# Six split-weight buffers per ring at one offset, constants in common tiles, a smaller DMA scratch, a re-priced plan, and short inverse roots on GpSimd

## Chip, core and metric

The kernel runs on one core of a Trainium2 chip. The time is the device time of one execution in microseconds (us). Lower is better. One execution of it was also recorded by the hardware profiler, and the rows below come from that recording.

## What is computed

Two layers of a hybrid block over 256 latent tokens and 256 context tokens, model width 1024, all in float32. Each layer normalises the tokens with a modulated RMS norm, projects them once, feeds three token mixers, merges these by gates, projects, and runs an MLP of width 4096. The last layer needs the latent tokens alone.

```python
for l in range(DEPTH):                                   # DEPTH = 2
    mod = silu(c) @ w_mod[l] + b_mod[l]                  # shifts, scales, gates
    h_lat, h_ctx = rms_norm(x, norm1_g[l]) * (1 + sc1) + sh1, ...   # 256 tokens each
    z = split_cols(h @ w_in[l])                          # one projection for all branches
    y_da  = rms_norm(differential attention over [lat, ctx]) # per head, q and k rms-normed, rope
    y_gla = rms_norm(gated linear attention, both ways) * silu(gate)
    y_na  = neighbourhood attention on a 64-wide grid (q, k rms-normed)
    m = sum(sigmoid(g_i) * (y_i @ w_br_i)) @ w_out[l]
    x = x + g1 * m
    x = x + g2 * (relu(h2 @ w_ff1[l]) ** 2) @ w_ff2[l]   # h2: second modulated norm
    if l < DEPTH - 1: the same for ctx                   # 512 columns in layer 0, 256 in layer 1
```

## The kernel before

All weights come from HBM in pieces of 128x1024 float32 (512 KB), in one planned list. For each piece `load_weights` issues a transfer on SyncE's queue (SP) into one of five `raw` buffers. `split_weights` then makes two float32r halves of it: ScalarE (ACT) copies it to `wh`, VectorE (DVE) subtracts to give `wl`. A product takes three float32r matmuls: high by high, high by low, low by high. There are five `wh` and five `wl` buffers (`NW`), each 1152 wide, and the piece's 1024 columns start at an offset that goes by the buffer: 0 for pieces planned without `shift`, and `SHIFTS` = 16, 48, 64, 80, 112 columns for those with it. Pieces with `shift` are those of layer 1 that TensorE (PE) holds as the stationary operand, with 256 columns moving: 24 of the gates, 12 of the branches, 8 of the output projection, 32 each of ff1 and ff2, 108 in all. In each of them 8 blocks by 3 products are 24 matmuls.

The order of the instructions is made while the program is built. `Lane` hands every instruction to `Plan.note`, which adds up planned times (`FIXED`, `PER`, `LATENCY`, `SLOWER`), and `drive` runs the tasks (first norm, modulation, norms, attention branches, the weight stream) by when their inputs will be there by that plan. Each engine then runs its own list in order. So a changed price in the plan changes the order on all engines.

An inverse root is made by `rsqrt` on DVE: a bit trick and three Newton steps, after one instruction that scales and adds EPS. It stands at the five norms over the model width (`norm_rms`; 4 columns in the first one, 2 in the others), at GLA's heads (`heads_rms` with 8 columns), at the end of each differential-attention head (`head_end`; 4 columns in layer 0, 2 in layer 1), and at the q and k of both softmax attentions (16 or 32 columns).

In each layer the job `ga` loads three tables: `sb` (gains and lambdas) and two `gl` tiles (decay bias and decay weights `a2`), on SP's queue. ACT and DVE split the second `gl` tile (tile `a`) and the decay projection `gat`, and PE needs both for the decays. The residual stream `x` is loaded again in layer 0 by eight transfers on GpSimd's (POOL's) queue.

Of the kernel before, what the change touches and what calls it, by code (L numbers as in the profile page):

```python
# [11 lines left out]
F32 = mybir.dt.float32  # L12
# [7 lines left out]
P = 128  # L20
# [16 lines left out]
OFF_GATE = (4640, 5664, 6688)  # L37


RS = -1.0 / 8192.0  # L40

SA_BMOD, SA_N1, SA_N2, SA_W = 0, 48, 56, 64
SB_GQ, SB_GQP, SB_GK, SB_GKP = 0, 64, 128, 192
SB_LAM = 256
SB_SUB, SB_GN, SB_NQ, SB_NK, SB_W = 512, 513, 514, 515, 516


INF = 1e9
# [12 lines left out]
AHEAD = 2
# [7 lines left out]
MOD1_AFTER = (0, "ff1", 0)  # L69


FIXED = {"DVE": 0.068, "ACT": 0.1, "Pool": 0.045, "PE": 0.005}
PER = {"DVE": 1.04e-3, "ACT": 0.833e-3, "Pool": 2.3e-3, "PE": 1 / 2400}
LATENCY = {"DVE": 0.13, "ACT": 0.2, "Pool": 0.13, "PE": 0.25, "DMA": 2.0}
DMA_PER_BYTE = 2.9 / 2 ** 20


class Plan:
# [13 lines left out]
    def note(self, lane, op, args, kw):  # L92
        aps = [x for x in args[1:] if isinstance(x, bass.AP)]
        aps += [v for k, v in kw.items() if isinstance(v, bass.AP) and k != "accum_out"]
        out = args[0]
        width = lambda x: math.prod(x.shape[1:])
        n = width(out)
        if op == "dma_start":
            us = n * out.shape[0] * 4 * DMA_PER_BYTE
            self.now["DMA"] = max(self.now["DMA"], self.now["PE"]) + us  # L100
            self.wr[out.tensor.name] = max(self.now["DMA"], self.rd.get(out.tensor.name, 0.0) + us) + LATENCY["DMA"]
            return
        if lane == "PE":
            passes = 2 if op == "transpose" else 1 if aps[0].dtype == F32R else 4
            us = max(n, 64) * passes * PER["PE"] * out.shape[0] * aps[0].shape[0] / P ** 2 * SLOWER[passes] + FIXED["PE"]
            shape = aps[0].shape[0], out.shape[0]
            kind = shape, passes
            us += SWITCH * (shape != self.kind[0]) + SWITCH * (kind != self.kind and kind == ((P, P), 1))
            self.kind = kind
        else:  # L110
            n = max(n, max((width(x) for x in aps), default=0))
            sb = lane == "DVE" and op in ("tensor_copy", "tensor_scalar", "memset") and \
                not any(x.tensor.name.startswith("ps") for x in aps)
            us = FIXED[lane] + n * PER[lane] * (0.5 if sb else 1)
            pointers = sum(width(x) == 1 for x in aps) if n > 1 else 0
            if lane == "ACT" and REFINE:
                us += 0.09 * (pointers + ("accum_out" in kw)) - (0.042 if aps[0].tensor.name.startswith("ps") else 0)
            elif lane == "ACT" and "accum_out" in kw:
                us += 0.09
            elif lane == "DVE" and REFINE and pointers:  # L120
                us += 0.06
        start = max(self.now[lane], self.ready(aps), self.rd.get(out.tensor.name, 0.0))
        end = start + us
        self.now[lane] = end
        for x in aps:
            self.rd[x.tensor.name] = max(self.rd.get(x.tensor.name, 0.0), end)
        for x in [out] + ([kw["accum_out"]] if "accum_out" in kw else []):
            self.wr[x.tensor.name] = end + LATENCY[lane]

# [30 lines left out]
def build(nc, tc, ctx, a):  # L160
# [63 lines left out]
    def after(key):  # L224
        return lambda: 0.0 if key in done else INF
# [23 lines left out]
        else:  # L249
            V.tensor_tensor(out, x, x, MULT)  # L250

    def rsqrt(dst, x, tmp):

        V.tensor_scalar(dst.bitcast(I32), x.bitcast(I32), -0.5, 1597463007.0, MULT, ADD)
        n = x.shape[-1]
        for thr in (3.0, 12.0, 768.0):
            if n <= 2:
                for i in range(n):
                    c = slice(i, i + 1)
                    V.scalar_tensor_tensor(tmp[:, c], dst[:, c], dst[:, c], x[:, c], MULT, MULT)  # L260
            else:
# [6 lines left out]
    raws, parts, held = {}, {}, []  # L270

    def plan_w(src, width=2048, shift=False):
# [10 lines left out]
    def split_weights(force=False):  # L283
# [14 lines left out]
        if held[-1]:  # L298
            w = []
            for c in cs:  # L300
                w.append((u("xw", dtype=F32R), u("xw", dtype=F32R)))
                S.activation(w[-1][0], s[:, c], AF.Copy)
                V.tensor_tensor(w[-1][1], s[:, c], w[-1][0].bitcast(F32), SUB)
        else:

            i = SHIFTS[st["ring"]] if plan[n][1] else 0
            st["ring"] = (st["ring"] + 1) % NW
            h, lo = [buf(t, t, 1152, NW, F32R)[:, i:i + 1024] for t in ("wh", "wl")]
            S.activation(h, s, AF.Copy)
            V.tensor_tensor(lo, s, h.bitcast(F32), SUB)  # L310
            w = [(h[:, c], lo[:, c]) for c in cs]
# [298 lines left out]
    def heads_rms(zs, width):  # L610
# [100 lines left out]
    def da_attn(L, lam_init, y):  # L711
        l, q, k, v = L["l"], L["dq"], L["dk"], L["dv"]
        nq = len(L["qt"])
        yield after((l, "dq"))
        sb = L["sb"]
        tab = []
        for (g0, g1, f) in ((SB_GQ, SB_GQP, RS * HD ** -0.5), (SB_GK, SB_GKP, RS)):
            t = small("ropet", [P, 2, 2, HD])
# [16 lines left out]
        V.tensor_scalar(gain, sb[:, SB_SUB:SB_SUB + 1], 0.5 * (1.0 - lam_init) * RS, None, MULT)  # L735
# [79 lines left out]
        def head_end(h, left):  # L815
# [8 lines left out]
            V.tensor_scalar(ss, ss, 1.0 / P, EPS, MULT, ADD)  # L824
            rsqrt(r, ss, tmp)
# [113 lines left out]
    def gla(L, y):  # L939
# [151 lines left out]
    def start(l, h):  # L1091
# [431 lines left out]
    def first_norm():  # L1523
# [18 lines left out]
        trif = u("trif").rearrange("p (r c) -> p r c", r=4)  # L1542
        S.dma_start(trif, a["tri"])
# [54 lines left out]
def _layout(i):  # L1598
# [52 lines left out]
    sb[:, :, SB_SUB] = i["da_subln_g"]  # L1651
    sb[:, :, SB_GN] = i["gla_gn_g"]
    sb[:, :, SB_NQ] = np.concatenate([i["na_qn_g"]] * 2, 1)
    sb[:, :, SB_NK] = np.concatenate([i["na_kn_g"]] * 2, 1)
# [29 lines left out]
```

## Time and profile before

| what | value |
|---|---|
| median of 3 runs | 1524.97 us (1524.93 to 1526.73) |
| profiled execution, own time | 1523.46 us |
| its span | 1521.3 us |
| PE busy | 1487.3 us (98%) |
| DVE, ACT, POOL busy | 1068.6, 707.2, 20.8 us |
| mean granted TensorE clock | 0.994 |

The profiled execution is 1.5 us under the median, and 2.2 us of it lie outside its span. Busy time is a union of records, and a matmul's record reaches past the start of the next one, so the pace of PE is read from the distance between starts.

### The profile page before, as it was taken

Reading aid. Unit: us, or ns where it says so; the run is one execution under the profiler, and the core shown is the slowest. Engines: PE = TensorE matmul, PEld = TensorE weight load, DVE = VectorE, ACT = ScalarE, POOL = GpSimd, SP = SyncE. Lnnn points to the kernel's source line nnn. Section 1 sums busy time; section 2 is a strip of 40 time slices with the busy share of each in tenths; the row PEclk is TensorE's granted clock in tenths of the full one; section 3 lists DMA queues with packets and bytes.
Section 4 is the critical chain, followed back from the end, with each engine's and each line's share of the span. In section 5 each row is a group of like instructions: output and inputs, shape, how many; then the busy total and the mean of one; then the engine's idle time right before and its main releaser. Section 6 shows DMA issues by size and latency. Waiting matters only on the chain.

```text
span 1521.3 us, 24039 instructions
## 1 busy us (share of the span) xinstructions
PE 1487.3 (98%) x9340; PEld 1279.3 (84%) x9340; DVE 1068.6 (70%) x2242; ACT 707.2 (46%) x1243; POOL 20.8 (1%) x30
## 2 busy tenths in 40 slices
PE   7899999999999999999999999999999999999999
PEld 5788878888877888988888888888887889989999
DVE  5788796698986376698876334877867685786543
ACT  4444435553345433623324252464466455477632
POOL 0100000000000100100000000000000000000000
PEclk9999999999999999999999999999999999999999
DMA  9533331157522422366885222324224325346662
GB/s 364 189 108 104 97 112 56 56 187 224 185 80 67 139 97 84 132 219 199 262 274 173 97 97 91 111 70 133 84 77 138 130 92 186 128 164 202 208 201 78
DMA packets 77793, 216.66 MB, mean 142 GB/s; under 512 B 9072, under 2 KB 12528, under 8 KB 77680
## 3 DMA queue, kind: packets, MB, share of 16 engines
q1 hardware_dynamic: 74880, 210.28, 41.7%
q10 hardware_dynamic: 2160, 2.76, 0.6%
q0 software_dynamic: 640, 2.10, 0.4%
q8 instruction: 73, 1.20, 0.3%
q14 instruction: 40, 0.33, 0.1%
HBM read 214.05 MB, written 1.05 MB: 141 GB/s over the span
## 4 chain that ended last, share of the span: by engine, by line
PE 75%; DVE 17%; ACT 3%; DMA 3%; issue 2%; SPq 0%; ACTq 0%; DVEq 0%
PE psg L141 63%; PE pss L141 11%; DVE wl L141 4%; DVE dump L141 2%; DVE z L141 2%; DVE wm L141 2%; DMA wm<-w_mod 2%; ACT wh L141 1%; DVE ss L141 1%; DMA gl<-gl 1%; DVE hn L141 1%; DVE h L141 1%; DVE S L141 1%; DVE st L141 0%; DMA raw<-w_tok 0%
## 5 line engine op out<-in xcount | busy, mean ns | idle before, releaser
L141 DVE TENSOR_TENSOR wl<-raw,wh 128x1024 fp32r<-128x1024 f32 x290 | 354.2, 1228 | 163.1 <-ACT wh L141 162.7
L141 PE MATMUL psg<-h,wh 128*128 128x256 f32 (+1 forms) x1808 | 444.4, 337 | 3.9 <-ACT z L141 2.0
L141 ACT ACTIVATE wh<-raw 128x1024 fp32r<-128x1024 f32 x290 | 301.7, 1053 | 195.3 <-PE psg L141 186.2
L141 PEld LDWEIGHTS psg<-h,wh 128*128 128x128 f32 x1808 | 305.6, 190 | 43.6 <-issue 5.5
L141 PE MATMUL psg<-wh,h 128*128 128x512 f32 (+1 forms) x1056 | 333.3, 391 | 0.1
L141 PE MATMUL psg<-h,wl 128*128 128x256 f32 (+1 forms) x904 | 301.4, 333 | 0.5 <-DVE wl L141 0.5
L141 PE MATMUL psg<-act,wh 128*128 128x256 f32 (+1 forms) x1056 | 249.0, 329 | 0.0
L141 PEld LDWEIGHTS psg<-wh,h 128*128 128x128 f32 x1056 | 197.7, 188 | 43.9 <-issue 2.5
L141 PE MATMUL psg<-wl,h 128*128 128x512 f32 (+1 forms) x528 | 204.3, 387 | 0.0
L141 PEld LDWEIGHTS psg<-act,wh 128*128 128x128 f32 x1056 | 178.3, 188 | 18.8
L141 PEld LDWEIGHTS psg<-h,wl 128*128 128x128 f32 x904 | 171.1, 189 | 18.1 <-DVE wl L141 0.8
L141 PE MATMUL psg<-act,wl 128*128 128x256 f32 (+1 forms) x528 | 173.9, 329 | 0.0
L141 DVE SCALAR_TENSOR_TENSOR dump<-wm,cb 128x512 f32<-128x512 f32 x160 | 107.8, 686 | 19.4 <-DMA wm<-w_mod 17.0
L141 PEld LDWEIGHTS psg<-wl,h 128*128 128x128 f32 x528 | 99.6, 189 | 18.9
L141 PEld LDWEIGHTS psg<-act,wl 128*128 128x128 f32 x528 | 99.4, 188 | 9.4
L141 PE MATMUL psg<-y,wh 128*128 128x512 f32 (+1 forms) x384 | 96.4, 342 | 0.0
L141 DVE TENSOR_TENSOR act<-r,act 128x256 fp32r<-128x256 f32 (+1 forms) x65 | 36.2, 557 | 66.9 <-ACT act L141 66.9
L141 DVE SCALAR_TENSOR_TENSOR x<-psg,mod,x 128x256 f32<-128x256 f32 x96 | 43.1, 479 | 56.7 <-PE psg L141 56.7
L141 ACT ACTIVATE r<-psg 128x256 f32<-128x256 f32 (+1 forms) x63 | 30.0, 476 | 95.8 <-PE psg L141 95.8
L141 PEld LDWEIGHTS psg<-y,wh 128*128 128x128 f32 x384 | 64.3, 189 | 7.3 <-issue 0.7
L141 PE MATMUL psg<-sp,wh 128*128 128x256 f32 (+1 forms) x304 | 66.5, 315 | 1.7 <-ACT sp L141 1.4
L141 DVE SCALAR_TENSOR_TENSOR wm<-wm,cb 128x512 f32<-128x512 f32 x96 | 66.2, 690 | 2.7
(223 smaller groups left out, 1679.4 us busy)
## 6 DMA issues: line engine op xcount, KB each, us to landing
raw<-w_ff SPq DMA_DIRECT2D x128, 512.0 KB, 4.4
wm<-w_mod SPq DMA_DIRECT2D x192, 256.0 KB, 4.0
raw<-w_tok SPq DMA_DIRECT2D x72, 512.0 KB, 4.0
raw<-w_gate SPq DMA_DIRECT2D x48, 512.0 KB, 3.9
raw<-w_br SPq DMA_DIRECT2D x24, 512.0 KB, 3.5
raw<-w_out SPq DMA_DIRECT2D x16, 512.0 KB, 3.8
tb<-natb SPq DMA_DIRECT2D x16, 192.0 KB, 4.1
x<-xc SPq DMA_DIRECT2D x8, 256.0 KB, 4.1
```

Source lines behind the costliest of these rows:

```text
L141: r = f(*args, **kw)
```

## The change

Six things are edited together. The rings get a sixth `wh` and `wl` buffer, and all shifted pieces start at column 16. Room for them comes from a DMA scratch of 1 KB in place of 4 KB, and from the differential-attention tables, which move to tiles of the common pool (`tabs`, `few`, and the 512 columns `sbd` of the table `sb`). `inv_rms` takes the place of `rsqrt`: up to 8 columns it is one DVE instruction and one GpSimd `pow` with exponent -0.5, above that Newton as before. The `gl` tiles are loaded from ACT's queue. The copy of the constant `tri` is made in layer 0's GLA, not at the start. The plan's prices change (a DMA's latency from 2.0 to 3.3, the factor of one-pass matmuls from 1.057 to 1.0622, a price for `pow`).

```diff
-RS = -1.0 / 8192.0
+RS = 1.0 / 8192.0
-NU, NRAW, NW, NWM = 64, 5, 5, 4
+NU, NRAW, NW, NWM = 64, 5, 6, 4
-SHIFTS = 16, 48, 64, 80, 112
+SHIFT = 16
-SWITCH, SLOWER = 0.095, {1: 1.057, 2: 1.0, 4: 1.03}
+SWITCH, SLOWER = 0.095, {1: 1.0622, 2: 1.01, 4: 1.05}
-LATENCY = {"DVE": 0.13, "ACT": 0.2, "Pool": 0.13, "PE": 0.25, "DMA": 2.0}
+LATENCY = {"DVE": 0.13, "ACT": 0.2, "Pool": 0.13, "PE": 0.25, "DMA": 3.3}
...
+            if ALU.pow in args:
+                us = 0.35 + 0.185 * n
...
-    def rsqrt(dst, x, tmp):
+    def inv_rms(dst, x, n, tmp, src=None):
+
+        src = x if src is None else src
+        m = x.shape[-1]
+        if m <= 8:
+            V.tensor_scalar(x, src, RS * RS / n, RS * RS * EPS, MULT, ADD)
+            G.tensor_tensor(dst, x, nhalf[:, :m], ALU.pow)
+            return
...
-            i = SHIFTS[st["ring"]] if plan[n][1] else 0
-            st["ring"] = (st["ring"] + 1) % NW
+            i = SHIFT if plan[n][1] else 0
             h, lo = [buf(t, t, 1152, NW, F32R)[:, i:i + 1024] for t in ("wh", "wl")]
...
-            L["sb"] = spool.tile([P, SB_W], F32, name=nm("sb"), tag="sb", bufs=1)
-            SP.dma_start(L["sb"], a["sb"][l])
+            L["sb"] = spool.tile([P, SB_W - 512], F32, name=nm("sb"), tag="sb", bufs=1)
+            SP.dma_start(L["sb"], a["sb"][l, :, 512:])
+            L["sbd"] = u("sbd")
+            SP.dma_start(L["sbd"], a["sb"][l, :, :512])
             ab, a2 = u("gl"), u("gl")
             for i, t in enumerate((ab, a2)):
-                SP.dma_start(t, a["gl"][l, i])
+                S.dma_start(t, a["gl"][l, i])
...
-        V.tensor_copy(tri, trif)
+        trif.append(u("trif").rearrange("p (r c) -> p r c", r=4))
+        S.dma_start(trif[0], a["tri"])
...
-    nc = bacc.Bacc("TRN2", target_bir_lowering=False, num_devices=1, dynamic_dma_scratch_size=4096)
+    nc = bacc.Bacc("TRN2", target_bir_lowering=False, num_devices=1, dynamic_dma_scratch_size=1024)
```

What this does to the order is shown at three places. The first is SP's queue in layer 0, where the first token projection is running and the tables of `ga` are due; the name in brackets is the semaphore that the issue waits for, and transfers take the eight DMAHW semaphores in turn. Before:

```order
L141 DMA raw_603<-w_tok 128x1024 [waits DMAHW3_49,DMAHW0_49,DVE_49]
L141 DMA wm_614<-w_mod 128x512 [waits DMAHW4_49]
L141 DMA wm_616<-w_mod 128x512 [waits DMAHW5_49]
L141 DMA wm_618<-w_mod 128x512 [waits DMAHW6_49]
L141 DMA wm_620<-w_mod 128x512 [waits DMAHW7_49]
L141 DMA sb_650<-sb 128x516 [waits DMAHW0_49]
L141 DMA gl_652<-gl 128x512 [waits DMAHW1_49,PE_49]
L141 DMA gl_653<-gl 128x512 [waits DMAHW2_49,PE_49]
```

And of the change, at the same place:

```order
L144 DMA raw_595<-w_tok 128x1024 [waits DMAHW3_49,DMAHW0_49,DVE_49]
L144 DMA raw_607<-w_tok 128x1024 [waits DMAHW4_49,DMAHW1_49,DVE_49]
L144 DMA wm_615<-w_mod 128x512 [waits DMAHW5_49]
L144 DMA wm_617<-w_mod 128x512 [waits DMAHW6_49]
L144 DMA wm_619<-w_mod 128x512 [waits DMAHW7_49]
L144 DMA wm_621<-w_mod 128x512 [waits DMAHW0_49]
L144 DMA sb_646<-sb 128x4 [waits DMAHW1_49]
L144 DMA sbd_648<-sb 128x512 [waits DMAHW2_49,PE_49]
```

One more `raw` transfer stands ahead of the modulation's weights (`wm`), and the two `gl` transfers have left the queue. They now stand on ACT. This is ACT at that place before, from the first of the four evacuations `z` of that projection:

```order
L141 ACTIVATE z_631<-psg_338 128x512 [waits PE_49]
L141 ACTIVATE z_636<-psg_368 128x512 [waits PE_49,Activation_49]
L141 ACTIVATE z_641<-psg_372 128x512 [waits PE_49,Activation_49]
L141 ACTIVATE z_648<-psg_376 128x512 [waits PE_49]
L141 ACTIVATE wh_665<-raw_336 128x1024 [waits Activation_49]
L141 ACTIVATE a_153_656<-gl_653 96x512 [waits DMAHW2_49]
L141 ACTIVATE gat_708<-psg_671 96x512 [waits PE_49]
```

And of the change:

```order
L144 ACTIVATE z_629<-psg_331 128x512 [waits PE_49]
L144 ACTIVATE z_634<-psg_350 128x512 [waits PE_49,Activation_49]
L144 ACTIVATE z_639<-psg_354 128x512 [waits PE_49,Activation_49]
L144 ACTIVATE z_644<-psg_358 128x512 [waits PE_49]
L144 DMA gl_650<-gl 128x512 [waits DMAHW3_49]
L144 DMA gl_651<-gl 128x512 [waits DMAHW4_49]
L144 ACTIVATE wh_667<-raw_377 128x1024 [waits Activation_49]
L144 ACTIVATE a_156_654<-gl_651 96x512 [waits DMAHW4_49]
L144 ACTIVATE gat_703<-psg_663 96x512 [waits PE_49]
```

The issues follow the four `z` on ACT and wait there for semaphores DMAHW3 and DMAHW4, which the two `raw` transfers of the SP list above hold until they land. The third place is DVE at a norm over 2 columns (`ms` is the mean square, `nr` its inverse root). This is the chain before, and the change has its first row and none of the others, with one GpSimd row `nr<-ms,nhalf` after it:

```order
L141 TENSOR_SCALAR ms_5849<-pss_5844 128x2 [waits PE_49]
L141 TENSOR_SCALAR nr_5851<-ms_5849 128x2 [waits DVE_49]
L141 SCALAR_TENSOR_TENSOR nt_5852<-nr_5851,ms_5849 128x1 [waits DVE_49]
L141 SCALAR_TENSOR_TENSOR nt_5852<-nr_5851,ms_5849 128x1
L141 SCALAR_TENSOR_TENSOR nr_5851<-nt_5852,nr_5851 128x2 [waits DVE_49]
```

The last three of these rows stand three times. In all, 16 such chains (5 norms, 8 heads, 3 times GLA's heads) leave DVE and 16 `pow` appear on GpSimd.

## Rows read from the trace of the kernel before

**Rows 1.** The page's first part: busy us (share of the span), instructions.

```profile
PE 1487.3 (98%) x9340; PEld 1279.3 (84%) x9340; DVE 1068.6 (70%) x2242; ACT 707.2 (46%) x1243; POOL 20.8 (1%) x30
```

**Rows 2.** Who waited for whom on PE: us in total, times, longest.

```profile
PE pss L141 <- DVE z L141: 3.9, 6, 1.4
PE pss L141 <- DVE gat L141: 3.0, 2, 2.2
...
PE psg L141 <- DVE wl L141: 1.4, 3, 0.5
...
PE pss L141 <- ACT dao L141: 1.3, 2, 0.9
...
PE pss L141 <- DVE rb L141: 0.6, 1, 0.6
```

**Rows 3.** Windows: busy PE, PEld, DVE, ACT, POOL; granted clock. Two slower stretches.

```profile
65.07:68.48 3.41, 3.41 (x9) 2.67 (x10) 3.31 (x5) 0.63 (x1) 0.00 (x0) 0.50 0.36 102
600.96:607.79 6.83, 6.33 (x28) 6.04 (x29) 6.54 (x20) 2.05 (x4) 0.00 (x0) 0.50 0.48 155
```

**Rows 4.** The chain that ended last, its last long piece.

```profile
1349.96 168.21 PE psg L141 x1442
```

**Rows 5.** Windows, columns as before, of five MLP pieces in a row, layer 1.

```profile
1406.21:1408.93 2.72, 2.72 (x26) 2.72 (x25) 1.54 (x3) 2.17 (x4) 0.00 (x0) 1.00 0.56 184
1408.93:1411.65 2.72, 2.72 (x26) 2.72 (x25) 1.65 (x3) 2.17 (x4) 0.00 (x0) 1.00 0.55 193
1411.65:1414.53 2.88, 2.88 (x27) 2.88 (x25) 1.82 (x3) 2.17 (x4) 0.00 (x0) 1.00 0.59 199
1414.53:1417.36 2.83, 2.83 (x26) 2.83 (x25) 1.60 (x3) 2.17 (x4) 0.00 (x0) 1.00 0.62 184
1417.36:1420.18 2.82, 2.82 (x26) 2.82 (x25) 1.64 (x3) 2.17 (x4) 0.00 (x0) 1.00 0.57 192
```

**Rows 6.** A window of one unshifted piece, 256 columns moving, layer 0.

```profile
582.00:584.88 2.88, 2.88 (x27) 2.88 (x25) 1.87 (x4) 1.06 (x2) 0.00 (x0) 1.00 0.00 0
```

**Rows 7.** SP's queue in layer 0: start us, us, what it issued.

```profile
32.78 20.62 SPq L141 DMA_DIRECT2D raw<-w_tok  x6
...
56.10 0.88 SPq L141 DMA_DIRECT2D gl<-gl  x2
```

**Rows 8.** ACT in layer 0, by time, with the idle time before.

```profile
62.06 0.63 ACT L141 ACTIVATE a<-gl 96x512 fp32r<-96x512 f32 x1 [4.74 <-DMA gl<-gl]
```

**Rows 9.** Usual length of DVE's subtraction wl, from the page's groups.

```profile
L141 DVE TENSOR_TENSOR wl<-raw,wh 128x1024 fp32r<-128x1024 f32 x290 | 354.2, 1228 | 163.1 <-ACT wh L141 162.7
```

**Rows 10.** Transfers: count, KB each, median us from issue to landing.

```profile
raw<-w_tok SPq DMA_DIRECT2D x72, 512.0 KB, 4.0
...
gl<-gl SPq DMA_DIRECT2D x4, 256.0 KB, 5.0
```

**Rows 11.** ACT and SP in layer 1 around the same tables, by time.

```profile
981.33 0.63 ACT L141 ACTIVATE a<-gl 96x512 fp32r<-96x512 f32 x1 [3.88 <-DMA gl<-gl]
...
975.70 0.43 SPq L141 DMA_DIRECT2D sb<-sb  x1
```

**Rows 12.** DVE, norm over 2 columns: first row, and row behind the chain.

```profile
603.25 0.15 DVE L141 TENSOR_SCALAR ms<-pss 128x2 f32<-128x2 f32 x1
...
605.39 0.29 DVE L141 COPY rb<-nr 128x256 f32<-128x256 f32 x1
```

**Rows 13.** POOL's longest group: busy us, mean ns of one, idle before.

```profile
L141 POOL TENSOR_TENSOR cb<-cb,cbt 128x512 f32<-128x512 f32 x8 | 11.7, 1477 | 466.1 <-DVE cbt L141 466.1
```

**Rows 14.** DVE and POOL in one stretch, by time.

```profile
638.87 2.31 DVE L141 TENSOR_TENSOR wl<-raw,wh 128x1024 fp32r<-128x1024 f32 x1
...
635.77 6.55 POOL L141 TENSOR_TENSOR cb<-cb,cbt 128x512 f32<-128x512 f32 x4 [127.18 <-DVE cbt L141]
```

**Rows 15.** Reloads of x: issue on POOL, first use on DVE.

```profile
504.16 4.43 POOL L141 DMA_DIRECT2D x<-xc  x8 [156.84 <-PE pss L141]
...
L141 DVE SCALAR_TENSOR_TENSOR x<-psg,mod,x x16: 474/478/484, 556.4 to 598.6; 128x256 f32<-128x256 f32 x16
```

More of the change, by code (lines that the diff above doesn't have):

```diff
@@ L44 @@
 SB_LAM = 256
-SB_SUB, SB_GN, SB_NQ, SB_NK, SB_W = 512, 513, 514, 515, 516
+SB_SUB, SB_GN, SB_NQ, SB_NK, SB_W = 0, 1, 2, 3, 516
 INF = 1e9
-NU, NRAW, NW, NWM = 64, 5, 5, 4
+NU, NRAW, NW, NWM = 64, 5, 6, 4
 HO, HF, HL = 3, 4, 3
@@ L69 @@
 MOD1_AFTER = (0, "ff1", 0)
-FIXED = {"DVE": 0.068, "ACT": 0.1, "Pool": 0.045, "PE": 0.005}
+FIXED = {"DVE": 0.068, "ACT": 0.1, "Pool": 0.045, "PE": 0.0006}
 PER = {"DVE": 1.04e-3, "ACT": 0.833e-3, "Pool": 2.3e-3, "PE": 1 / 2400}
-LATENCY = {"DVE": 0.13, "ACT": 0.2, "Pool": 0.13, "PE": 0.25, "DMA": 2.0}
+LATENCY = {"DVE": 0.13, "ACT": 0.2, "Pool": 0.13, "PE": 0.25, "DMA": 3.3}
 DMA_PER_BYTE = 2.9 / 2 ** 20
@@ L250, in square @@
             V.tensor_tensor(out, x, x, MULT)
-    def rsqrt(dst, x, tmp):
-        V.tensor_scalar(dst.bitcast(I32), x.bitcast(I32), -0.5, 1597463007.0, MULT, ADD)
-        n = x.shape[-1]
-        for thr in (3.0, 12.0, 768.0):
[L257 to L263, printed above, removed]
+    def inv_rms(dst, x, n, tmp, src=None):
[5 more added lines that the diff above has]
+            return
+        V.tensor_scalar(x, src, 1.0 / n, EPS, MULT, ADD)
+        V.tensor_scalar(dst.bitcast(I32), x.bitcast(I32), -0.5, 1597463007.0 - 2.0 ** 31, MULT, ADD)
+        for thr in (3.0, 12.0, 768.0):
+            V.tensor_tensor(tmp, dst, dst, MULT)
+            V.tensor_tensor(tmp, tmp, x, MULT)
             V.scalar_tensor_tensor(dst, tmp, -thr, dst, ADD, MULT)
     plan = []
-    st = {"load": 0, "split": 0, "cur": 0, "more": 0, "raw": 0, "room": 0, "hold": 0, "ring": 0}
+    st = {"load": 0, "split": 0, "cur": 0, "more": 0, "raw": 0, "room": 0, "hold": 0}
     raws, parts, held = {}, {}, []
@@ L396, in build @@
     tri = const("tri", [P, 4, P], F32R)
+    nhalf = const("nhalf", [P, 8])
+    V.memset(nhalf, -0.5)
     ind = const("ind", [P, P])
@@ L405, in build @@
     scl = [[const(f"scl{l}{n}", [P, KT, 2]) for n in range(2)] for l in range(DEPTH)]
+    trif = []
     def mod_scale(l, n, k0, k1, ns=2):
@@ L485, in norm_rms @@
         ms = small("ms", [P, 4])
-        V.tensor_scalar(ms[:, :nt], ps.rearrange("p (t c) -> p t c", c=P)[:, :nt, 0], 1.0 / D, EPS, MULT, ADD)
         r = small("nr", [P, 4])
         tmp = small("nt", [P, 4])
-        rsqrt(r[:, :nt], ms[:, :nt], tmp[:, :nt])
+        inv_rms(r[:, :nt], ms[:, :nt], D, tmp[:, :nt], ps.rearrange("p (t c) -> p t c", c=P)[:, :nt, 0])
         rb = u("rb").rearrange("p (t c) -> p t c", c=P)
@@ L619, in heads_rms @@
         yield need(ss, lane="DVE")
-        V.tensor_scalar(ss, ss, 1.0 / width, EPS, MULT, ADD)
         r = small(f"sr{n * g}", [P, n * g])
         tmp = small(f"st{n * g}", [P, n * g])
-        rsqrt(r, ss, tmp)
+        inv_rms(r, ss, width, tmp)
         return r.rearrange("p (n g) -> p n g", g=g)
@@ L714, in da_attn @@
         yield after((l, "dq"))
-        sb = L["sb"]
-        tab = []
+        sb, few, tabs, tab = L["sbd"], u("few"), u("tabs"), []
         for (g0, g1, f) in ((SB_GQ, SB_GQP, RS * HD ** -0.5), (SB_GK, SB_GKP, RS)):
-            t = small("ropet", [P, 2, 2, HD])
+            t = tabs[:, 256 * len(tab):][:, :256].rearrange("p (a t d) -> p a t d", a=2, t=2)
             V.tensor_tensor(t[:, 0], rope[:, 0], sb[:, g0:g0 + HD].unsqueeze(1).to_broadcast([P, 2, HD]), MULT)
@@ L722, in da_attn @@
             V.tensor_scalar(t2, t2, f, None, MULT)
-            gc = small("gainc", [P, HD])
+            gc = few[:, HD * len(tab):][:, :HD]
             V.tensor_scalar(gc, sb[:, g0:g0 + HD], f, None, MULT)
             tab.append((t, gc))
-        lp = small("lp", [P, 2, HD], 1)
+        lp = few[:, 2 * HD:4 * HD].rearrange("p (a d) -> p a d", a=2)
         sl = sb[:, SB_LAM:SB_LAM + 4 * HD].rearrange("p (a b d) -> p a b d", a=2, b=2)
@@ L734, in da_attn @@
         gain = small("dgain", [P, 1], 1)
-        V.tensor_scalar(gain, sb[:, SB_SUB:SB_SUB + 1], 0.5 * (1.0 - lam_init) * RS, None, MULT)
+        V.tensor_scalar(gain, L["sb"][:, SB_SUB:SB_SUB + 1], 0.5 * (1.0 - lam_init) * RS, None, MULT)
         h8 = lambda x: x.rearrange("p (h d) -> p h d", d=HD)
@@ L823, in head_end @@
             yield need(ss, lane="DVE")
-            V.tensor_scalar(ss, ss, 1.0 / P, EPS, MULT, ADD)
-            rsqrt(r, ss, tmp)
+            inv_rms(r, ss, P, tmp)
             for t in range(0, nq, 2):
@@ L962, in gla @@
             las[t] = split(la[t])
+        if l == 0:
+            copy(tri, trif[0])
         yield after((l, "gv"))
@@ L1541, in first_norm @@
             S.dma_start(dst, a[n])
-        trif = u("trif").rearrange("p (r c) -> p r c", r=4)
-        S.dma_start(trif, a["tri"])
-        V.tensor_copy(tri, trif)
+        trif.append(u("trif").rearrange("p (r c) -> p r c", r=4))
+        S.dma_start(trif[0], a["tri"])
         mskf = u("mskf")[:, :2 * P].rearrange("p (r c) -> p r c", r=2)
@@ L1650, in _layout @@
     o["gl"] = gl
[L1651 to L1654, printed above, removed]
+    sb[:, :, 512 + SB_SUB] = i["da_subln_g"]
+    sb[:, :, 512 + SB_GN] = i["gla_gn_g"]
+    sb[:, :, 512 + SB_NQ] = np.concatenate([i["na_qn_g"]] * 2, 1)
+    sb[:, :, 512 + SB_NK] = np.concatenate([i["na_kn_g"]] * 2, 1)
     o["sb"] = sb
```

## The prediction, made before the changed kernel ran

> **What bounds the kernel now.** The page's first part comes first: TensorE (PE) is busy 1487.3 us of the span of 1521.3, DVE 1068.6, ACT 707.2, POOL 20.8 [rows 1]. Time can be won where PE waits, where its clock is low, and where its matmuls follow each other slower than they could. The list of who waited for whom on PE is read next: the largest entries are DVE's `z` with 3.9 us and `gat` with 3.0, then `wl` 1.4, ACT's `dao` 1.3 and the norms' `rb` 0.6 [rows 2]; all of PE's waits together are 1521.3 − 1487.3 = 34 us, start and end included. Then the granted clock. It is 1.00 nearly everywhere and 0.50 (1.2 in place of 2.4 GHz) in four stretches, each behind waits of PE: one is 3.41 us long, one 6.83 [rows 3], and two more are as long as the first. Work in them takes twice its time, so each of the three short ones costs 1.7 us and the long one 3.4, 8.5 in all.
>
> The third place is in PE's steady work. The chain that ended last has 168.21 us of uninterrupted PE work in its last piece, 1442 matmuls of layer 1's MLP [rows 4]. Windows cut at the starts of its 24-matmul pieces (the first number is the window's length) give 2.72, 2.72, 2.88, 2.83 and 2.82 us, at one clock, with PE never idle and no trend in DVE, ACT or DMA share [rows 5]. The period is five, the number of offsets in `SHIFTS`, and in the order of the program the five stand at columns 16, 48, 64, 80 and 112. So the place of the stationary operand is worth up to 0.16 us a piece. An unshifted piece of layer 0, at column 0 with 256 columns moving, takes 2.88 too [rows 6].
>
> **The change part by part.**
>
> *One offset.* Every shifted piece would then stand at column 16. A sixth buffer of 1152 columns (4608 bytes, nine times 512) keeps the place of column 16 the same, counted in steps of 512 bytes, in every buffer; that is why I take the pace of the first two windows for all. The mean of the five windows is 13.97/5 = 2.794, so a piece gains 0.074. The 1442 matmuls are 60 pieces, worth 4.4 us. The other 48 of the 108 pieces would give up to 3.6 more; they lie between waits, some of them at a pace that fits the pattern less well, and I count 2.0. **−6.4** (−4.4 to −8.0).
>
> The Trainium skill ("TensorE: Matmul & The Clock Gate", "Step-by-step: what each phase is for") says that PE reads moving and stationary operands through two independent SBUF ports, so that loading the next weights takes nothing from the matmul that runs. By that rule the offset is worth 0. The windows speak against it, since nothing but the weights' place has their period.
>
> *Loads of `gl`, layer 0.* Before, SP issues the sixth `raw` of its group at about 32.78 + 20.62 = 53.4 and the two `gl` from 56.10 [rows 7]; ACT waits 4.74 us for the second and makes `a` at 62.06 [rows 8]. Now the two issues stand on ACT behind four `z` and wait for the semaphores of the sixth and seventh `raw`. The seventh comes when a buffer is free, one `wl` of 1.228 us later [rows 9]: 54.6, plus 4.0 to its landing is 58.6, plus 5.0 for `gl` [rows 10] is 63.6, against 62.06. That is 1.5 late. Queued behind the waiting issues on ACT are a `wh`, `a` and ACT's `gat`, for which PE waits; on DVE an evacuation that stood between `a` and `gat` moves behind, 0.7 back. **+0.8** (−1 to +3).
>
> *Loads of `gl`, layer 1.* There the semaphores are free, and `sb`, 0.43 us on SP, no longer stands ahead of them; ACT waited 3.88 us for `gl` [rows 11], and of PE's 3.0 us for `gat`, 2.2 are layer 0's [rows 2], so 0.8 bounds it. **−0.5** (0 to −0.8).
>
> *Inverse roots.* A norm's chain runs on DVE from 603.25 to 605.39, 2.14 us, eleven instructions, of which the first, 0.15, stays [rows 12]. The trace has no `pow`. From below it is the small DVE instruction, 0.15; from above POOL's 128x512 product, 1.477 [rows 13]. The price that the diff gives its planner for two columns, 0.72, lies between, and I take it, nearer the upper row since a root is more than a product per element. With handoffs to POOL and back the chain is some 1.1 in place of 2.14, by the bounds 0.6 to 1.9. PE cannot get back more than it waits: `rb`, 0.6, and `dao`, 1.3, which stands behind the head's root [rows 2]. I take **−0.6** and, with half of `dao`'s wait not the root's, **−0.8** (together 0 to −1.9).
>
> *DVE's load.* Sixteen chains at some 1.95 us leave DVE, 31 us. POOL gets 8 `pow` of 2 columns, 5 of 4 and 3 of 8, by the same price 8×0.72 + 5×1.09 + 3×1.83 = 17 us. While POOL ran `cb`, a DVE subtraction lasted 2.31 [rows 14] where 1.228 is usual [rows 9]: what POOL holds, DVE may lose, so about 14 net. The Trainium skill ("SBUF — State Buffer", "SBUF: two separate sides") has this as an exclusive lock on a port pair; these two rows agree. DVE was idle 30% of the time, so most of the 14 is worth nothing, and it counts only where PE waited for DVE (`z` 3.9 [rows 2]). **−1.5** (0 to −6).
>
> *Sixth pair of buffers.* It lets a split run one piece further ahead. In the order of the program this moves little at the end of layer 0, and it can take at most the waits for `wl`, 1.4 [rows 2]. **−0.7** (0 to −1.4).
>
> *At nothing.* Moving `tri`'s copy puts one instruction of 0.6 us, by the row of `a` on ACT [rows 8], where ACT waits for other things; without that cover it is 0.6. Tables in common tiles change addresses, not instructions; one more transfer for `sb`, 0.43 on SP [rows 11], lies between loads that wait for buffers. The smaller scratch can slow POOL's queue, which carries the reloads of `x`: issued from 504.16, first used at 556.4 [rows 15]. One after the other at 4 us each (as `raw`, twice as large or more [rows 10]) they are there by 541, 15 us early; without that cover each would delay the residual sums by up to 4.
>
> *New plan.* The prices move many rows by a place on PE. The trace can't say where a wait arises; one stretch at half clock more or less is 1.7. I take **+1.0** (−3 to +4).
>
> **Sum.** −6.4 + 0.8 − 0.5 − 0.6 − 0.8 − 1.5 − 0.7 + 1.0 = −8.7: a span of 1512.6. The profiled execution had 2.2 outside its span (1514.8), and the median of the runs lies 1.5 above it: **1516**.
>
> **The rivals.**
>
> *The waits go too.* If DVE's 14 us and the new order take most of what PE waits for (`z`, `gat`, `wl`, `dao`, `rb`: 10.2 in all [rows 2]), say 9.0, two short stretches at half clock go with them, since each follows such waits [rows 3]: −6.4 − 9.0 − 3.4, a span of 1502.5, **1506**. For it: the waits are short. Against it: `gat`'s is for a transfer that doesn't get faster.
>
> *The offset is not the cause.* If the pace goes with something else of period five (the `raw` ring had five buffers too, and keeps them), the 6.4 falls away: **1522.4**, no change. Against it: the unshifted piece is as slow as the one at column 64 [rows 6].
>
> *Slower: `pow` is long.* Thirteen chains (five norms, eight heads) end in work that PE waits for, with nothing else to hold it. The Newton steps that go and the handoffs that come balance at a `pow` of about 1.8 us. Without the gains of roots and DVE the time is 1516 + 2.9 = 1518.9, and each us of `pow` above 1.8 adds 13. It decides from (1528 − 1518.9)/13 + 1.8 = 2.5 us; at 4 us the time is **1547**. For it: no row shows the operation, and POOL's plain product is already 1.477 [rows 13]. Against it: that product has 512 columns, the roots 2 or 4.
>
> **How the numbers follow.** Chances: the forecast 0.60, with a range of its own of 1511 to 1521; waits go too 0.18; the offset is not the cause 0.14; `pow` is long 0.08. About 0.2%, 3 us, is what a measurement of this kernel can tell from no change: faster is below 1521.9, slower above 1528. The forecast and the first rival are faster, 0.78, with a little of the second, 0.02; the rest of that is no change, 0.12; slower 0.08. The range takes in the first rival and the second with the lower half of its scatter: 1507 to 1525; outside stay `pow`'s case and the ends of the others.
>
> **What the changed profile would show.** The offset: windows of five successive pieces in layer 1's MLP all at 2.72; at 2.8 or 2.88 the step is wrong. `gl`: ACT's `a<-gl` in layer 0 near 63.6 (later than 66 or earlier than 61 is wrong), PE's wait for `gat` near 4. Roots: sixteen `pow` rows on POOL, at two columns 0.4 to 1.2 us; about 145 instructions fewer on DVE; waits for `rb` and `dao` under 1 us. `wl`'s waits under 1. The reloads of `x`: no PE wait that leads back to POOL's queue. Three to five stretches at half clock; more, or new waits of over 5 us in all, make the forecast wrong on the side of the time before.

## The result and the profile after

| | before | changed |
|---|---|---|
| median (runs, range) | 1524.95 us (4, 1521.49 to 1526.73) | 1503.72 us (4, 1502.47 to 1509.61) |
| ratio, 95% interval | | 0.987 (0.9844 to 0.9897) |
| profiled execution: time, span | 1523.46, 1521.3 | 1502.47, 1500.7 |
| mean granted clock | 0.994 | 0.998 |

The kernel became faster by 21 us where 9 were forecast; the time lies under the range. In a later set of runs the changed kernel took 1507.69 us in the median of six (1503.63 to 1512.29), 0.9887 of before; why it scatters so is told under run 3.

The spans differ by 20.6 us. The page's first part of the changed kernel answers to [rows 1]:

```profile
PE 1472.2 (98%) x9340; PEld 1268.0 (84%) x9340; DVE 1036.4 (69%) x2069; ACT 709.7 (47%) x1247; POOL 38.3 (3%) x47
```

Outside PE's busy time 1500.7 − 1472.2 = 28.5 us are left, 5.5 less than before; the other 15.1 are inside it. First the pace: the chain that ended last has the same 1442 matmuls as in [rows 4], 4.48 us shorter:

```profile
1333.41 163.73 PE psg L144 x1442
```

Windows of two successive pieces of it, to be held against [rows 5], both show 2.72 (length, then busy PE, PEld, DVE, ACT, POOL, granted clock, DMA):

```profile
1404.37:1407.09 2.72, 2.72 (x26) 2.72 (x25) 1.65 (x3) 2.18 (x4) 0.00 (x0) 1.00 0.62 185
1407.09:1409.81 2.72, 2.72 (x26) 2.72 (x25) 1.65 (x3) 2.17 (x4) 0.00 (x0) 1.00 0.62 200
```

Taken over all shifted pieces, from the distances between starts, the time above 113.33 ns a matmul fell from 7.4 to 1.2 us. Second the clock. Beside the two of [rows 3], the kernel before had two stretches at half clock in layer 1:

```profile
1116.38:1119.79 3.41, 3.41 (x15) 2.44 (x15) 2.04 (x2) 2.56 (x5) 0.00 (x0) 0.50 0.55 173
1310.93:1314.35 3.42, 3.42 (x18) 3.42 (x18) 2.32 (x6) 1.77 (x3) 0.00 (x0) 0.50 0.58 187
```

Windows at the places of [rows 3] in the changed kernel:

```profile
65.68:69.09 3.41, 3.36 (x8) 2.68 (x9) 2.58 (x7) 0.00 (x0) 0.00 (x0) 0.50 0.33 96
596.58:603.41 6.83, 5.36 (x42) 4.91 (x41) 4.40 (x8) 3.35 (x4) 0.70 (x1) 1.00 0.44 144
```

The first is still at half clock; the second runs at full clock, and the two in layer 1 are gone too. If work at half clock took twice its time, that would be (6.83 + 3.41 + 3.41)/2 = 6.8 us. It does not quite; here is PE inside the stretch of 6.83 us, before:

```profile
602.63 0.63 PE L141 MATMUL pss<-h,wh 128*128 128x256 f32 x2
603.06 0.41 PE L141 MATMUL pss<-h,wl 128*128 128x256 f32 x1
603.27 0.63 PE L141 MATMUL psg<-h,wh 128*128 128x256 f32 x2
```

Three matmuls take 0.64 us, 213 ns each, against 120 at full clock [rows 6], which makes it 6.0. So 5.5 of waits, 6.2 of pace and 6.0 to 6.8 of clock make some 18 of the 20.6; the rest is spread. The waits of PE that answer to [rows 2] (us in total, times, longest):

```profile
PE psg L144 <- DVE gat L144: 4.3, 1, 4.3
PE psg L144 <- DVE wl L144: 2.0, 3, 0.8
...
PE pss L144 <- DVE z L144: 1.6, 2, 1.0
```

`z` fell from 3.9 to 1.6, `dao` and `rb` are gone, `gat` rose from 3.0 to 4.3, and `wl` from 1.4 to 2.0. Two more waits are gone that [rows 2] does not list, for DVE's `e` in layer 1's attention and for ACT's `sp` in layer 1's merge. Before, they were:

```profile
PE pss L141 <- DVE e L141: 2.1, 1, 2.1
...
PE psg L141 <- ACT sp L141: 1.4, 1, 1.4
```

ACT and SP in layer 0, by time, answering to [rows 7, 8]:

```profile
33.03 20.48 SPq L144 DMA_DIRECT2D raw<-w_tok  x7
...
55.83 3.54 ACTq L144 DMA_DIRECT2D gl<-gl  x2
...
63.62 0.63 ACT L144 ACTIVATE a<-gl 96x512 fp32r<-96x512 f32 x1 [3.15 <-DMA gl<-gl]
```

The norm of [rows 12], on DVE and POOL by time:

```profile
599.83 0.15 DVE L144 TENSOR_SCALAR ms<-pss 128x2 f32<-128x2 f32 x1
600.80 0.29 DVE L144 COPY rb<-nr 128x256 f32<-128x256 f32 x1 [0.82 <-POOL nr L144]
...
600.06 0.70 POOL L144 TENSOR_TENSOR nr<-ms,nhalf 128x2 f32<-128x2 f32 x1 [12.59 <-DVE ms L144]
```

From `ms` to `rb` the chain takes 0.97 us in place of 2.14. All `pow`, from POOL's groups (busy us, mean ns of one, idle before):

```profile
L144 POOL TENSOR_TENSOR der<-des,nhalf 128x4 f32<-128x4 f32 (+1 forms) x8 | 6.8, 853 | 248.7 <-DVE des L144 135.3 <-ACT pt L144 113.5
L144 POOL TENSOR_TENSOR sr<-ss,nhalf 128x8 f32<-128x8 f32 x3 | 6.4, 2149 | 186.0 <-DVE ss L144 186.0
...
L144 POOL TENSOR_TENSOR nr<-ms,nhalf 128x2 f32<-128x2 f32 (+1 forms) x6 | 4.5, 756 | 589.5 <-DVE ms L144 589.5
```

They are 17, not 16: the norm over the model width stands not five times but six, once with 4 columns and five times with 2.

### The profile page after: what moved, and what is told of

Its sections match the earlier page's. It is cut to its first block, busy times and chain, and to the rows that moved or that the text cites. A ratio compares the mean times of both kernels' runs of the same rounds, so it can differ in the third digit from the quotient of the medians.

```text
span 1500.7 us, 23880 instructions
## 1 busy us (share of the span) xinstructions
PE 1472.2 (98%) x9340; PEld 1268.0 (84%) x9340; DVE 1036.4 (69%) x2069; ACT 709.7 (47%) x1247; POOL 38.3 (3%) x47
## 4 chain that ended last, share of the span: by engine, by line
PE 74%; issue 12%; DVE 8%; DMA 3%; ACT 2%; POOL 0%; ACTq 0%; SPq 0%; POOLq 0%; DVEq 0%
PE psg L144 64%; PE pss L144 9%; DVE wl L144 2%; DMA wm<-w_mod 2%; DVE z L144 1%; DVE hn L144 1%; ACT wh L144 1%; DVE S L144 1%; DVE h L144 1%; DVE ss L144 1%; DVE rope L144 0%; DVE y L144 0%; DMA raw<-w_tok 0%; DVE st L144 0%; ACT h L144 0%
## 5 line engine op out<-in xcount | busy, mean ns | idle before, releaser
L144 PE MATMUL psg<-h,wh 128*128 128x256 f32 (+1 forms) x1808 | 439.2, 335 | 2.8 <-ACT z L144 1.1
L144 ACT ACTIVATE z<-psg 128x512 f32<-128x512 f32 (+1 forms) x60 | 35.0, 591 | 69.9 <-PE psg L144 60.2
```

The costliest lines, as they stand in the source:

```text
L144: r = f(*args, **kw)
```

## The experiments

The theory after the result: the pace of the shifted pieces (6.2 us), waits (5.5) and the half-clock stretches behind them (6 to 7) add up; the waits went because roots left DVE. Rivals for the waits: the plan's new prices, or the sixth buffer. All times are medians; before, on the same chips, took 1522.9 to 1525.6.

### The place of the weights

**1. The kernel before, all offsets at 16.** The order stays that of before.

```diff
-SHIFTS = 16, 48, 64, 80, 112
+SHIFTS = 16, 16, 16, 16, 16
```

> The kernel before with all five offsets at 16 and nothing else; the order of every engine's instructions is that of before. If the offset alone sets the pace of the shifted pieces, all 108 run at 2.72 us in place of a mean of 2.79: 8.0 us less, about 1517 against 1525, with the waits and the half-clock stretches where they were. If the pace goes with another ring of five, the windows keep their period and the time stays within 3 us of 1525. If shorter pieces move the work against DVE's deadlines, more waits appear and the gain is under 6.

1523.69 us, ratio 1.0001 (0.9985 to 1.0016): in the median, nothing. But the fastest of the 12 runs, the one with a profile, took 1515.17, and its last piece of the chain is 163.73 us long. The other eleven lie between 1520.2 and 1527.7. Their mean clocks, 0.996 to 0.998, are those of the fastest, 0.997, so half-clock stretches do not make the difference; no profile shows them, and 3 says what is likely in them.

**2. The changed kernel with its offset at 64.**

```diff
-SHIFT = 16
+SHIFT = 64
```

> The changed kernel with its one offset at 64 in place of 16, same order. If the offset sets the pace, each of 108 pieces takes 2.88 in place of 2.72: 17.3 us more, 1521 against 1503.7. If it does not, the time stays at 1504.

1518.28 us (1516.61 to 1518.88), 11 to 15 above the changed kernel. A window of one piece is 2.88, and the chain's 1442 matmuls take 9.57 us longer:

```profile
1338.91 173.30 PE psg L144 x1442
```

The place does set the pace, and 64 holds it at 120 ns.

**3. The changed kernel again.** No edit.

> The changed kernel itself, for the scatter of its time. Theory: in an uninterrupted stretch of layer 1's shifted pieces PE keeps one of two paces from start to end, 113.3 or 117.8 ns for a matmul of 256 columns, and which one is settled where the stretch begins; over the 60 pieces of the last stretch that is 60 x 24 x 4.45 ns = 6.4 us. Then single runs stand in two groups some 6 us apart, near 1503.5 and near 1509.5. Rival: the pace is fixed by the offset, and runs scatter by half-clock stretches alone, in steps of 1.7 us around one centre.

1503.63, 1503.79, 1505.62, then 1509.76, 1510.25, 1512.29: two groups. The clock does not part them: its mean is 0.996 in the lower three and 0.997, 0.996 and 0.996 in the upper. In the first runs, too, 1509.61 came with 0.998, as 1502.47 did. Neither its first profile nor this one caught the upper group, but those of three kernels with all pieces at 16 did (6, 8 and 10 below). Here is the last piece of the chain in 6, the same order of PE rows as the changed kernel's:

```profile
1348.12 170.12 PE psg L144 x1442
```

Two windows of it, 93 us apart, have one pace, 2.83:

```profile
1402.05:1404.88 2.83, 2.83 (x27) 2.83 (x26) 1.66 (x3) 2.17 (x4) 0.00 (x0) 1.00 0.50 174
1495.21:1498.04 2.83, 2.83 (x27) 2.83 (x25) 1.71 (x2) 1.06 (x1) 0.00 (x0) 1.00 0.13 46
```

At column 16 a matmul takes 113.3 or 117.8 ns, and in the profiles the last long piece keeps one of them throughout: 170.12 − 163.73 = 6.4 us, the distance of the two groups. That the upper group of this kernel is the slower pace is inferred from that; no profile of the kernel itself shows it. In the kernel before, 80 and 112 stand behind 64 and run at 117.8, and each passage from 112 to 16 brings 113.3 back [rows 5]. That is what the next two use.

**4. The changed kernel with one buffer of six at 112**, run twice, on two chips.

```diff
-SHIFT = 16
+SHIFTS = 112, 16, 16, 16, 16, 16
...
-            i = SHIFT if plan[n][1] else 0
+            i = SHIFTS[st["ring"]] if plan[n][1] else 0
+            st["ring"] = (st["ring"] + 1) % NW
```

> The changed kernel with one of its six buffers at 112 and five at 16, same order. In the kernel before each passage from 112 to 16 put the pace at 113.3. If this passage sets it, no stretch stays at 117.8 for longer than one turn of the ring, and the upper group of runs is gone: all near 1503 to 1505. If pieces at 112 run at 117.8 by themselves, 10 of the 60 pieces are slow and the time is 1 us above the lower group. If the passage does nothing, both groups are there as in the changed kernel.

> The kernel with one buffer at 112 once more, on the chip of this group of runs: 1503.5 to 1505, one group of times.

1504.18 us (1503.6 to 1505.11) and 1504.94 (1502.64 to 1506.82, wider than was expected): none of these eight runs lies above 1507, where four of the changed kernel's ten lie above 1509. The 1442 matmuls take 163.73 us in both profiles, so pieces at 112 run at 113.3 among the others. This kernel is the yardstick for what follows.

**5. The kernel before with one buffer of five at 112, four at 16.**

```diff
-SHIFTS = 16, 48, 64, 80, 112
+SHIFTS = 112, 16, 16, 16, 16
```

> The kernel before with one of its five buffers at 112 and four at 16, same order on every engine. All at 16 left the median where it was, since most runs kept the pace of 117.8 ns. If the passage from 112 to 16 restores 113.3 and the offset's gain is the 6 us that the first term of the sum said, the runs lie in one group near 1517 to 1518, against 1523.5 of before. If the changed kernel's better pace came from its order and not its offsets, the time stays above 1521.

1516.45 us, ratio 0.9953 (0.9937 to 0.9969): 7.0 us, in the order of before. The place alone is worth that, if the pace is held.

### The short roots

**6. Newton steps in place of `pow`, the plan left as it is**. The last piece and the windows in 3 are this run's.

```diff
-            V.tensor_scalar(x, src, RS * RS / n, RS * RS * EPS, MULT, ADD)
-            G.tensor_tensor(dst, x, nhalf[:, :m], ALU.pow)
+            V.tensor_scalar(x, src, 1.0 / n, EPS, MULT, ADD)
+            v = nc.vector
...
+                v.scalar_tensor_tensor(dst, tmp, -thr, dst, ADD, MULT)
+            pl.note("Pool", "tensor_tensor", (dst, x, nhalf[:, :m], ALU.pow), {})
```

> The changed kernel with Newton steps on DVE in place of the 16 pow, the planner still charging the price of pow, so that PE, ACT and SP keep their order row for row and DVE differs in the chains alone. If the short roots and DVE's relief took the waits and with them the half-clock stretches, 8 to 13 us come back (1512 to 1517) and PE waits for z, e, dao or rb as before. If the new order took them, no more than 3 us come back (to 1507).

1522.2 us (1518.68 to 1527.66). In its profile 6.4 us of this are the slower pace of 3. For the rest, PE waited for what stands behind the roots:

```profile
PE pss L144 <- DVE rb L144: 3.3, 4, 1.0
PE pss L144 <- ACT dao L144: 3.2, 4, 1.4
...
PE pss L144 <- DVE go L144: 2.3, 3, 0.9
```

**7. Newton steps, known to the planner**, first with all pieces at 16, then with one buffer at 112.

```diff
-        if m <= 8:
+        if m <= 0:
```

> The changed kernel with Newton steps in place of pow, this time known to the planner, which makes its order anew. With the order made for pow and Newton in its place PE waited 14.7 us longer (rb, dao, go, sg). If those waits came because the order counted on short roots, the planner hides most of them and 4 to 7 us remain against the changed kernel. If the length of the chains and DVE's load are what costs, 12 to 15 remain.

> The changed kernel with one buffer at 112 (one pace in all runs) and Newton steps in place of pow, known to the planner. At 1504.2 with pow. If short roots are worth what the held order showed, 8 to 14 us come back. If the planner covers the longer chains with other work, as the waits for rb and dao of 0 without pow say, 1 to 4 us: 1505 to 1508.

1509.02 and 1508.18 us. Beside the yardstick on its chip (1504.94) the second (1507.23 to 1509.55) is 3.2 above. PE waits neither for `rb` nor for `dao`: the planner put other work ahead. So 6 showed what an order that counts on short roots loses without them, not what the roots gave; the theory that they took the waits falls. But the new order has a wait of its own, in PE's list of the second run:

```profile
PE pss L144 <- DVE h L144: 4.2, 3, 3.8
```

The 3.8 us stand near 614, where DVE does four `act` of the MLP, each behind ACT, before it makes the `h` that PE needs. The wait for `gat` is 2.0 shorter than the yardstick's in return (3.4). In all, PE is idle for 29.9 us here and for 30.5 in the yardstick's profile. So what Newton and the order that was made for it cost together, 3.2 us, does not lie in the sum of PE's waits; where it lies is open.

### The plan's prices

**8. The old prices**, with all pieces at 16, then with one buffer at 112.

```diff
-SWITCH, SLOWER = 0.095, {1: 1.0622, 2: 1.01, 4: 1.05}
+SWITCH, SLOWER = 0.095, {1: 1.057, 2: 1.0, 4: 1.03}
...
-FIXED = {"DVE": 0.068, "ACT": 0.1, "Pool": 0.045, "PE": 0.0006}
+FIXED = {"DVE": 0.068, "ACT": 0.1, "Pool": 0.045, "PE": 0.005}
...
-LATENCY = {"DVE": 0.13, "ACT": 0.2, "Pool": 0.13, "PE": 0.25, "DMA": 3.3}
+LATENCY = {"DVE": 0.13, "ACT": 0.2, "Pool": 0.13, "PE": 0.25, "DMA": 2.0}
```

> The changed kernel with the plan's old prices for PE and DMA (latency 2.0, one-pass factor 1.057, 0.005 fixed), pow's price kept. If the new prices took the waits at z, e and sp with their half-clock stretches, 5 to 9 us come back. If the roots took them, within 3 us of the changed kernel.

> The changed kernel with one buffer at 112 and the plan's old prices. With the old prices PE waited 5.0 us for z in place of 1.7, and 2.5 for gat in place of 5: about 1 us by waits. If the prices bring only that, 1504 to 1507. If they decide the half-clock stretches too, 1507 to 1511.

1509.85 us in two groups (1507.23 to 1516.46), then 1509.97 in one (1509.65 to 1510.31), 5.0 above the yardstick. PE waits for `z` longer than in the kernel before, and a stretch at half clock of 6.83 us falls among two of these waits, of 1.4 us each, near 414 and 417:

```profile
PE pss L144 <- DVE z L144: 5.1, 6, 1.4
PE pss L144 <- DVE gat L144: 2.8, 2, 2.5
```

```profile
415.80:422.63 6.83, 5.63 (x21) 4.60 (x21) 5.16 (x7) 2.57 (x4) 0.00 (x0) 0.50 0.73 249
```

The first fence is PE's list of waits, the second a window, both of the second run. The new prices took 3.1 us of `z` (2.0 in the yardstick's profile) and gave 2.6 to `gat` (5.4 there): what they brought is mostly clock. PE is idle as long in both profiles (30.4 and 30.5 us), but busy at half clock for 12.5 us against 4.0, worth some 4 of the 6.1 us between their spans. The mean clock is 0.995 in all four runs, against 0.996 to 0.998 in the yardstick's.

### The sixth buffer

**9. Five buffers, one of them at 112.**

```diff
-NU, NRAW, NW, NWM = 64, 5, 6, 4
+NU, NRAW, NW, NWM = 64, 5, 5, 4
...
+SHIFTS = 112, 16, 16, 16, 16
```

> The changed kernel with five wh and wl buffers in place of six, one of them at 112. Every other part taken back so far left PE's waits for e (2.1 us before) and for sp (1.4) at 0. If the sixth buffer took them, 3.5 us come back, with one or two half-clock stretches of 1.7 us: 1508 to 1511 against 1504.2 with six. If the wait for wl was all that it was worth, 0.7 and no more: 1505.

1510.81 us (1510.14 to 1511.21), ratio 0.9912 against the yardstick's 0.9866 and 0.9876 on other chips: 5.5 to 7.0 us. The two waits are back, in PE's list of this run:

```profile
PE pss L144 <- DVE e L144: 2.1, 1, 2.1
...
PE psg L144 <- ACT sp L144: 1.6, 1, 1.6
```

PE by time shows why, first with five buffers, then in the yardstick:

```profile
1110.39 0.60 PE L144 MATMUL pss<-ident,e 128*128 128x128 f32 x4
1113.13 0.63 PE L144 MATMUL pss<-ident,e 128*128 128x128 f32 x4 [2.13 <-DVE e L144]
```

```profile
1098.13 0.60 PE L144 MATMUL pss<-ident,e 128*128 128x128 f32 x4
1098.48 0.49 PE L144 MATMUL psg<-h,wh 128*128 128x256 f32 x2
...
1098.92 0.39 PE L144 MATMUL psg<-y,wh 128*128 128x256 f32 x2
...
1100.97 0.60 PE L144 MATMUL pss<-ident,e 128*128 128x128 f32 x4
```

Between two softmax tiles lie some 3 us of DVE and ACT. With six buffers a branch piece (`psg<-y`) is split already and fills them; with five PE has nothing, since the next split ends only at 1114.11 on DVE:

```profile
1112.89 1.22 DVE L144 TENSOR_TENSOR wl<-raw,wh 128x1024 fp32r<-128x1024 f32 x1
```

With five buffers there is also a wait of 1.8 us for ACT's `z`, and a stretch at half clock right behind it:

```profile
PE psg L144 <- ACT z L144: 2.9, 2, 1.8
```

```profile
1067.30:1070.70 3.40, 3.40 (x9) 2.65 (x9) 2.06 (x4) 2.67 (x5) 0.00 (x0) 0.50 0.00 0
```

Of the 7.3 us between the spans of this profile and the yardstick's, 3.3 are idle time of PE, and some 2.8 come from its being busy at half clock for 9.9 us in place of 4.0. `wl`, the ring's own wait, is 2.0 with five buffers and with six.

### The late `gl`

**10. Both `gl` on SP's queue, ahead of `sb` and `sbd`**, where their semaphores are free.

```diff
+            ab, a2 = u("gl"), u("gl")
+            for i, t in enumerate((ab, a2)):
+                SP.dma_start(t, a["gl"][l, i])
             L["sb"] = spool.tile([P, SB_W - 512], F32, name=nm("sb"), tag="sb", bufs=1)
...
-            ab, a2 = u("gl"), u("gl")
-            for i, t in enumerate((ab, a2)):
-                S.dma_start(t, a["gl"][l, i])
```

> The changed kernel with both gl transfers on SyncE's queue again, ahead of sb and sbd, so that they take semaphores that are free. If the wait for the two raw transfers' semaphores is what made gl late, they are issued at about 55.5, land by 60.5, ACT's a stands near 61 in place of 63.6, and PE's wait for gat of 4.3 us falls to about 2: 1.5 to 2.5 us less, 1501.5. If ACT's queue or the transfer's own 5 us make the wait, nothing changes (within 1 us of 1503.7).

1510.46 us (1509.03 to 1511.83), with the pace of 117.8 in its profile; if all its runs have that pace, it is near 1504 without those 6.4 us, so the time tells nothing. The trace does: `gl` was issued at 57.22, ACT's `a` stood at 65.01, and PE waited 4.2 us for `gat`: free semaphores did not help. The queue ahead, and the 2 MB of `raw` and `wm` just issued, are what is left of the reasons; this run does not part them.

**11. `gl` issued ahead of the seven `raw`, one buffer at 112.**

```diff
         while st["load"] < len(plan) and st["raw"] < st["room"]:
+            if plan[st["load"]][0] is gl0[0] and len(gl0) == 1:
+                for i in range(2):
+                    gl0.append(u("gl"))
+                    SP.dma_start(gl0[-1], a["gl"][0, i])
```

> The changed kernel with one buffer at 112, and layer 0's two gl transfers issued at about 32 us, ahead of the seven raw transfers. If the load of the queues by raw and wm is what made gl late, ACT's a stands before 60, PE's wait for gat of 4.3 us goes, and the half-clock stretch at 65 with it: 4 to 6 us less than 1504.2, near 1499. If a and gat wait for something else (PE's own product for the decays), less than 1 us.

1502.9 us, ratio 0.9862: not to be told from the yardstick. ACT made `a` at 54.84, but DVE, by time, did this:

```profile
59.07 0.69 DVE L144 SCALAR_TENSOR_TENSOR dump<-wm,cb 128x512 f32<-128x512 f32 x1 [2.50 <-DMA wm<-w_mod]
...
61.22 0.68 DVE L144 TENSOR_TENSOR a<-gl,a 32x512 fp32r<-32x512 f32 x1
61.94 0.69 DVE L144 SCALAR_TENSOR_TENSOR wm<-wm,cb 128x512 f32<-128x512 f32 x1
...
62.67 0.68 DVE L144 TENSOR_TENSOR gat<-psg,gat 32x512 fp32r<-32x512 f32 x1
```

DVE waits 2.50 us for `wm`, with `a` and `gat` behind it. PE still waited 3.0.

**12. As 11, layer 0's pieces shifted too.**

```diff
-            i = SHIFTS[st["ring"]] if plan[n][1] else 0
+            i = SHIFTS[st["ring"]]
```

> As the run before, with layer 0's pieces shifted too (their place was column 0). Layer 0 has some 425 of these matmuls with 256 columns moving, at 119.9 ns; at 113.3 to 117.8 they give 0.9 to 2.8 us, and pieces with 512 columns moving, 227 ns each, nothing. If a place other than column 0 also slows something, such as the split, the time rises.

1515.47 us, 12.6 slower. PE by time, from the middle of a projection with 512 columns moving (rows of two `wh` alternate with rows of one `wl`):

```profile
699.97 0.63 PE L144 MATMUL psg<-h,wh 128*128 128x512 f32 x2
...
702.77 0.63 PE L144 MATMUL psg<-h,wh 128*128 128x512 f32 x2
```

Twelve matmuls in 2.80 us, 233 ns each, where run 11 has 227. PE, ACT, DVE and POOL keep the order of run 11. With 512 columns moving, column 0 is a better place than 16 or 112.

**13. As 11, with layer 0's modulation products let in only behind the decay projection.**

```diff
-            yield after("consts" if l == 0 else MOD1_AFTER)
+            yield after((0, "ga") if l == 0 else MOD1_AFTER)
```

> With one buffer at 112, gl early, and layer 0's modulation products let in only when the decay projection is done. With gl early alone ACT had made a at 54.8, but on DVE a and gat stood behind three products that waited for wm, and PE still waited 3.0 us. If this row order is what was left, PE's wait for gat falls under 1 us and the half-clock stretch at 63 goes: 3 to 5 us less than 1502.9 to 1504. If the half-clock stretch stays, 2.

1498.22 us (1497.97 to 1499.17), ratio 0.9831 (0.9813 to 0.9849), 6.7 under the yardstick beside it and faster than both kernels. From PE's waits, and from the view of the cores (span, mean clock):

```profile
PE psg L144 <- DVE gat L144: 0.5, 1, 0.5
```

```profile
core 0: 1496.2 us, clock 1.000
```

The wait that the change had lengthened is gone, and but for the last instants no stretch is at half clock any more.

## Why the prediction was wrong

Two terms of its sum failed. **Sixth pair of buffers**: −0.7 was bounded by the waits for `wl`, 1.4. Run 9 shows 5.5 to 7. A split in store does not only spare a wait for itself; it is work that PE has while it waits for something else, here `e` and `sp`, which the sum never named. They stood in PE's list with 2.1 and 1.4 us when the prediction called `z`, `gat`, `wl`, `dao` and `rb` its largest entries. The sign given for this term, waits for `wl` under 1 us, failed too: they are 2.0, with the sixth buffer and without. **New plan**: +1.0 was a guess about churn; run 8 shows −5.0. Both terms left the half-clock stretches where they were, and these were nearly a third of the difference: three to five were forecast, and but for the last 1.4 us the changed profile has one.

**One offset**: −6.4, and the profiles show 6.2; with the pace held, run 5 shows 7.0. The size was right, the reason only in part: column 16 allows 113.3 ns and does not secure it, and the median of run 1 got nothing. The rule that loading the next weights takes no SBUF read bandwidth from the matmul that runs (the Trainium skill, "TensorE: Matmul & The Clock Gate", "Step-by-step: what each phase is for") was read as giving 0; 163.73 against 173.30 us for 1442 matmuls, with the weights' place as the one difference, decide against that 0. Whether a load then takes something from the matmul or only lasts longer itself (its record is 192 ns at column 64, 188 at 16), no run parts.

**Loads of `gl`**: `a` was forecast at 63.6 and stood at 63.62; the wait for `gat` near 4, and it was 4.3. The reason given, two semaphores, is not borne out by run 10, where `a` stood later without them, so the hit is in part luck. Layer 1's part went as said: its wait of 0.8 for `gat` is gone. **Inverse roots and DVE's load**: `pow` on two columns 0.72 by the diff's price, 0.70 measured; the chain 1.1, measured 0.97. Together the terms said −2.9, and run 7 shows 3.2, but that agreement is luck: the terms put it on PE's waits for `rb`, `dao` and `z`, and with Newton in its own order PE is idle no longer than with `pow`. DVE lost 173 instructions, not 145: the 17 chains lost ten each, and three others went. **At nothing**: no wait of PE leads to POOL's queue or to `x`; the scratch, the tables and `tri` were not run by themselves.

Run by run the parts come to 7.0 + 3.2 + 5.5 to 7.0 + 5.0 = 20.7 to 22.2 us, where the yardstick's ratios say 19 to 20; they overlap a little. Of the rivals the first, that the waits go too (1506), came nearest. It put them on DVE's 14 us and the new order; the prices bear out the second half, and the sixth buffer stood in neither. Its 9.0 of waits and two short stretches also stand against 5.5 measured and three stretches, one of them long, so its nearness is in part luck. What sets the pace at column 16 stays open, and so does when a stretch at half clock follows: with the same waits of 0.5, 0.7 and 0.8 us near 597 to 600 the changed kernel's profile has none there, and its second one (run 3) has one of 3.41 us.

## What to carry to other kernels

A buffer more on a ring is costed by what the waiting engine could do in its other waits, not by the waits for that ring. Where an engine is 98% busy, look at its pace piece by piece, and trust the time of a single run only after seeing whether the runs lie in two groups. Undoing a part with the rest of the order held fast measures how much the order leans on it; undoing it with a new order measures what it is worth, together with what that order happens to cost.

## What was not expected of the hardware

A matmul of 256 columns in float32r held one of two paces, 113.3 or 117.8 ns, through 164 or 170 us with its weights at column 16, and 120 at column 64; a passage from 112 to 16 came with the faster. With 512 columns moving the weights at 16 or 112 took 229 to 234 ns (medians by group) and at column 0 227. POOL's `pow` took 0.70 us for 2 columns, 1.0 for 4, and 2.0 to 2.5 for 8.
